# One core, a hybrid decoder block: queries and keys stored two heads at a time, head loads from a high/low layout, gate squares in tiles of their own

## The chip, the cores and the metric

The kernel runs on one core of a Trainium2 chip, in one launch. The metric is the device time of one execution in microseconds (us). Below, PE is TensorE (matmuls), DVE is VectorE, ACT is ScalarE, POOL is GpSimd, and SP is the engine that issues nearly all DMAs. A DMA issued on SP or ACT goes through that queue's share of the core's 16 DMA engines. P is 128, the number of partitions. "Landing" is the time from the issue of a DMA to the moment when its last byte is there.

## What is computed

One decoder block on x of 1024 tokens by 1024 channels, float32. Cut to what matters here:

```python
xn = rmsnorm(h, norm_mix_g)
proj = xn @ w_in                      # q, k, v (8 heads x 64), u, vg (512 each), 8 forget gates
log_f = log_sigmoid(proj[..., G_END:] + b_forget)
att = forgetting_attention(q, k, v, log_f)   # softmax(q k / 8 + c_q - c_k, causal) v; c = cumsum(log_f)
uv = gelu(proj[..., V_END:G_END])
sg = u * (causal 128x128 mix of rmsnorm(vg, per group of 64))
h = h + concat(att, sg) @ w_out
h = h + conv_ffn(rmsnorm(h, norm_ffn_g))     # 1024 -> 5632, width-3 convolution, silu gate, 2816 -> 1024
out = rmsnorm(h, norm_final_g)
```

## The kernel before

Float32 products are made from a high and a low part: a value is cast to a shorter format (high), the rest is the low part, and three matmuls (high x high, high x low, low x high) make one product. The big products are also split by Strassen's scheme in 2x2 blocks, hence names such as A11, S2, T4 for sums of blocks. The work runs in stages:

- 0 to 100 us: the gate half of the first projection (`tmul`, `tprod`; matmuls at L542) with x transposed, which comes in by `load_x` and a first tile `xg` (first 512 columns of x and the gain). `own` makes the parts of x. The weights `wuv` come through SP, the first through ACT's queue.
- 100 to 200 us: forget gates (`forget`, L745 to L774, and `forget_sums`), then four query and key steps (`qk_step`, L887 to L931; matmuls in `product`, L691). Step i makes the transposed queries and keys of heads 2i and 2i+1: tiles of 128 partitions by 1024 tokens. `emit` (L832 to L839) scales them, splits them and stores both parts to DRAM, half a row (512 tokens) at a time. Between the steps' parts, `gate(n)` runs a few pieces of `gate_work` (L799 to L821): squares of the gate half into a "pt" tile (ACT), sums over groups (DVE, L806), square root, and the two multiplications of each tile (L818, L820).
- 200 to 400 us: the values' product (L542), the spatial mix (L971 to L973), and eight heads of attention. Head h needs A (queries, high and low in 128 partitions), B (keys, high and low), B2 (keys, low and high) and ck (the forget sums, the same in each partition). `head_loads` (L852 to L860) brings them by five DMAs into tiles with tags "x1" and "x2", two of each, so that the loads of one head can run while another is computed. `logits` (L1051, L1052) needs all of A, B and B2 for its first block. Beside the heads, PE makes the gated half's output product piece by piece (`Gated`, L1167): each unit of 128 tokens loads a piece of x (L1148) into one of two halves of a tile, adds into it and stores it (L1178) to `hpd`.
- 400 to 1060 us: the rest of the output product, the FFN in blocks, the final norm.

DRAM holds the queries and keys as `qd` and `kd`, shape [8, 2, 64, 1024]: head, high or low, dimension, token. A head's A and B are one contiguous block of 512 KB there.

The order of the instructions on each engine is set by a planner, class `Pace` (L33 to L336): it is given each instruction's cost (`cost`, L143) and a due time worked back from PE, and lists the instructions of each engine in the order in which they would run (`run`, L278). The program then keeps that order; each engine works in order, and waits only where data or a tile require it. So a change of the costs moves instructions on all engines.

Of the kernel before, what the change touches and what calls it, by code (L numbers as in the profile page):

```python
# [14 lines left out]
P = 128  # L15
# [17 lines left out]
class Pace:  # L33
# [109 lines left out]
    def cost(self, i, eng):  # L143

        def size(a):
            n = 1
            for s, c in list(a.ap)[1:]:
                n *= c
            return n

        ins = [a for a in i.ins if getattr(a, "bass_ap", None) is not None]
        outs = [a for a in i.outs if getattr(a, "bass_ap", None) is not None]
        sb = lambda a: a.bass_ap.tensor.name in self.slot and not self.psum(a)
        n = size(outs[0]) if outs else 1
        kind = type(i).__name__
        if "DMA" in kind:
            b = max(size(a) * list(a.ap)[0][1] * 4 for a in ins + outs)
            return 60 if eng == "SP" else 270, b / 330.0 + (1700 if b > 1 << 16 else SMALL), b / 330.0
        if eng == "PE":
            m = size(ins[0])  # L160
            w = size(ins[1])
            exact = "float32r" not in str(ins[0].dtype) and "float32" in str(ins[0].dtype) and not i.is_transpose
            c = 4 * max(m / 2.4, 25) + 230 if exact else max(m / 2.4 + 13.4, w / 1.2 + 2)
            return c, m / 2.4 + 176, 0
        ptr = sum(1 for a in ins if size(a) == 1 and n > 1)
        if eng == "DVE":
            if getattr(i, "is_tensor_tensor_scan", False):
                return 2.1 * n + 100, 2.1 * n + 180, 0
            if "Custom" in kind:
                return n / .96 + 212, n / .96 + 292, 0  # L170
            if "Reduce" in kind:
                return size(ins[0]) / .96 + 70, size(ins[0]) / .96 + 150, 0
            if "Reciprocal" in kind:
                return 150 + 6 * n, 150 + 6 * n, 0
            full = [a for a in ins if size(a) > 1 or n == 1]
            if "TensorTensor" not in kind and len(full) < 2 and not ptr:
                d = n / (1.92 if all(sb(a) for a in ins + outs) else .96) + 150
            else:
                d = n / .96 + 146 + (60 if ptr else 0)
            return d - 80, d, 1 if sum(1 for a in full if size(a) > 8 and sb(a)) >= 2 else 0  # L180
        if eng == "ACT":
            d = n / 1.2 + (160 if any(self.psum(a) for a in ins) else 195) + 100 * ptr
            return (d + 95, d + 190, 0) if len(outs) > 1 else (d - 100, d, 0)
        if "TensorTensor" in kind:
            return 2.0 * n + 160, 2.17 * n + 180, 1
        return .85 * n + 180, .85 * n + 180, 1
# [91 lines left out]
    def run(self, ops, succ, due):  # L278
# [6 lines left out]
        port = {"DVE": 0.0, "POOL": 0.0}  # L285
        order = {e: [] for e in can}
        start = [0.0] * n
        bus, table, done, end = 0.0, 0, 0, 0.0
        for k in range(n):
            if not left[k]:  # L290
                can[ops[k][1]].append(k)
        while done < n:
            pick = None
            for e, ks in can.items():
                if not ks:
                    continue
                f = max(free[e], bus - BACKLOG) if e == "SP" else free[e]
                soon = min(max(f, ready[k]) for k in ks)
                k = min((k for k in ks if ready[k] <= soon + LOOK[e]), key=lambda k: (due[k], k))
                s = max(f, ready[k])  # L300
                if pick is None or s < pick[0]:
                    pick = (s, k)
            s, k = pick
            i, e, (cad, lat, x), deps, fn = ops[k]
            turn = e == "TURN"
            can[e].remove(k)
            if fn and fn != table:
                s += 1283 if table else 0
                table = fn
            if e in port and x:  # L310
                s = max(s, port["POOL" if e == "DVE" else "DVE"])
                port[e] = s + cad
            dma = "DMA" in type(i).__name__
            free[e] = s + cad
            if dma:
                bus = max(s + 300, bus) + x
                fin = bus + lat - x - 200
            else:
                fin = s + lat
            start[k] = s  # L320
            end = max(end, fin)
            if not turn:
                order[e].append(k)
            done += 1
            for q in succ[k]:
                r = s if turn or ops[q][1] == "TURN" else s + cad if ops[q][1] == e and not dma else fin + HOP
                if r > ready[q]:
                    ready[q] = r
                left[q] -= 1
                if not left[q]:  # L330
                    can[ops[q][1]].append(q)
        return order, start, end


SLACK, BACKLOG, SMALL = 30000.0, 3000.0, 4500.0
LOOK = {"PE": 0.0, "DVE": 0.0, "ACT": 0.0, "POOL": 0.0, "SP": 0.0, "TURN": 0.0}  # L336


# [1 line left out]
def block_kernel(ctx: ExitStack, tc: tile.TileContext, xT, xtok, wuv, wv, wqk, wf, cpk, xg, bfv,  # L340
# [81 lines left out]
    bcol = cst.tile([64, 2], F32, name="bcol")  # L422


    qd = drm.tile([8, 2, 64, 1024], F32, name="qd")
    kd = drm.tile([8, 2, 64, 1024], F32, name="kd")
    rbd = drm.tile([8, P], F32, name="rbd")
    ncd = drm.tile([8, 1024], F32, name="ncd")
    zd = drm.tile([8, 1024], F32, name="zd")
# [34 lines left out]
    def gk(k, neg=False):  # L464
        return (ng1 if neg else g1)[:, k:k + 1]

    def xr(n, k):
        return RAW[n][k // 2][:, k % 2, 0:512]

    def load_x(n, k, row, hf):  # L470
        sp.dma_start(out=xr(n, k), in_=xT[row * P:(row + 1) * P, hf * 512:hf * 512 + 512])
# [12 lines left out]
    def own(n, src, k, row, cuts=(0, 512), g=None):  # L484

        g = gk(row) if g is None else g

        for a, b in zip(cuts, cuts[1:]):
            act.activation(xs(n, 0, k)[:, a:b], src[:, a:b], AF.Copy, scale=g)
        dve.scalar_tensor_tensor(out=xs(n, 1, k), in0=src, scalar=g, in1=f32(xs(n, 0, k)),  # L490
                                 op0=ALU.mult, op1=ALU.subtract)

    def hl_of(n, j, src):
        act.copy(x2(n, 0, j), src)
# [6 lines left out]
    gb = []  # L501
    for k in range(4):
        if k == 0:
            sp.dma_start(out=RAW["x11"][0][:, 0, :], in_=xg)
        else:
            load_x("x11", k, k, 0)
        (sp if k else act).dma_start(out=ua[k][:, 0, :], in_=wuv[k, :, 0, :])
    for k in range(4):
        load_x("x21", k, 4 + k, 0)
        sp.dma_start(out=ua[k][:, 1, :], in_=wuv[k, :, 1, :])  # L510
# [43 lines left out]
    for k in range(4):  # L554
        w = tsplit(ua[k][:, 0, :], hi_eng="act" if k else "dve")
        if k == 0:
            graw = RAW["x11"][0][:, 0, 512:520]
            own("B11", xr("x11", 0), 0, 0, (0, 128, 512), graw[:, 0:1])
            dve.tensor_copy(g1, graw)
            dve.tensor_scalar(out=ng1, in0=g1, scalar1=-1.0, scalar2=None, op0=ALU.mult)  # L560
        else:
            own("B11", xr("x11", k), k, k)
        tmul(B, w, "B11", k, True, apart=(k == 0))
    for k in range(4):
        own("B21", xr("x21", k), k, 4 + k)
        tmul(S, tsplit(ua[k][:, 1, :]), "B21", k, True)
    for m in range(4):
        act.copy(vgt[0][:, m, :], B[m])
    for j in range(2):
        dve.tensor_tensor(out=tmp[j][0], in0=RAW["x11"][j][:, :, 0:512], in1=RAW["x12"][j], op=ALU.subtract)  # L570


    def values_low(k):
# [171 lines left out]
    def forget():  # L745
# [16 lines left out]
        for hf in range(2):  # L762
# [7 lines left out]
            zh = zr[:, hf * 512:hf * 512 + 512]  # L770
            act.copy(zh, ps[32:40, :])
            dve.tensor_tensor(out=zh, in0=ps[0:8, :], in1=zh, op=ALU.add)
            pool.tensor_tensor(out=zh, in0=zh, in1=rb[0:8, hf * 512:hf * 512 + 512], op=ALU.mult)
        sp.dma_start(out=zd, in_=zr)  # L774

    def forget_sums():
# [19 lines left out]
    gms = cst.tile([P, 64], F32, name="gms")  # L796
    gg = []

    def gate_work():  # L799

        for hf in (1, 0):
            for t in (0, 2):
                sq = sb("pt", [P, 2, 512])
                act.activation(sq, vgt[hf][:, t:t + 2, :], AF.Square)
                r = gms[:, hf * 32 + t * 8:hf * 32 + t * 8 + 16]
                dve.tensor_reduce(out=r, in_=sq.rearrange("p t (g d) -> p (t g) d", d=64), axis=AX.X, op=ALU.add)  # L806
# [19 lines left out]
        for _ in range(n):  # L826
            next(gw, None)

    gate(2)
    tq, tk = sb("G", [P, 2, 1024]), sb("G", [P, 2, 1024])  # L830

    def emit(t, dst, i, scale, parts):  # L832
        for o in parts:
# [1 line left out]
                                     op0=ALU.mult, op1=ALU.mult)  # L835
            act.copy(t[:, 0, o].bitcast(F32R), t[:, 1, o])
            dve.tensor_tensor(out=t[:, 1, o], in0=t[:, 1, o], in1=t[:, 0, o], op=ALU.subtract)
            for j in range(2):
                sp.dma_start(out=dst[2 * i + j].rearrange("s d t -> d s t")[:, :, o], in_=t[j * 64:(j + 1) * 64, :, o])  # L839

    vgs = []

# [9 lines left out]
    def head_loads(h):  # L852
        ab, nb = sb("x1", [P, 2, 1024], F32R), sb("x2", [P, 2, 1024], F32R)
        A, B, ck, B2 = ab[:, 0, :], ab[:, 1, :], f32(nb[:, 0, :]), nb[:, 1, :]
        sp.dma_start(out=f32(A), in_=qd[h].rearrange("s d t -> (s d) t"))
        sp.dma_start(out=f32(B), in_=kd[h].rearrange("s d t -> (s d) t"))
        sp.dma_start(out=f32(B2[0:64, :]), in_=kd[h, 1])
        sp.dma_start(out=f32(B2[64:128, :]), in_=kd[h, 0])
        sp.dma_start(out=ck, in_=ncd[h:h + 1, :].to_broadcast((P, 1024)))
        return A, B, ck, B2  # L860

# [936 lines left out]
def layouts(inp):  # L1798
# [18 lines left out]
    wos = w_out[512:].reshape(2, 2, P, 2, 512).transpose(3, 0, 2, 1, 4)  # L1817

    wu = g["w_up"][0].reshape(2, 4, P, 2, NFF, P).transpose(4, 2, 3, 0, 1, 5)[:, :, ::-1].reshape(NFF, P, 4, 512)
    r = {"xT": x.T, "xtok": x, "wuv": uv, "wv": wv, "wqk": qk, "wf": wf, "cpk": cpk, "xg": np.concatenate([x.T[:P, :512], g["norm_mix_g"][0].reshape(8, P).T], axis=1),  # L1820
         "bfv": np.repeat(g["b_forget"][0], 8).reshape(64, 1), "ggain": g["gmlp_norm_g"][0].reshape(1, 512),
         "g2r": g["norm_ffn_g"][0].reshape(1, 1024), "gfr": g["norm_final_g"].reshape(1, 1024),
         "wsp": g["w_spatial"][0].transpose(2, 0, 1), "woa": woa, "wos": wos, "wup": wu, "wdn": g["w_down"][0]}
# [17 lines left out]
```

## Time and profile before

| What | us |
|---|---|
| median of three runs (1061.94, 1062.12, 1063.27) | 1062.12 |
| the profiled execution's own time | 1062.15 |
| its span (first to last instruction) | 1060.4 |
| landing of a head's A load (512 KB), median | 4.1 |
| landing of its B load (512 KB), median | 5.6 |
| landing of one half of B2 (256 KB), median | 6.7 |
| landing of its ck load (512 KB), median | 7.5 |
| landing of a queries' store (256 KB, 16 of them), median | 8.5 |
| landing of a keys' store (256 KB, 16 of them), median | 3.7 |

The 1.75 us between the span and the time of the execution lie outside the instructions. In the profile's rows an engine's line is "start, duration, engine, line, operation, out<-in, count", with the idle time before it and what ended it in brackets. In the table of waits a row has the total, the number of times and the longest. In the rows by stage each engine has its busy time and number of instructions, then come the granted PE clock (1.00 is full), the share of time that the 16 DMA engines were busy, and GB/s. DMA packets are what one DMA engine moves at once (a row of 4 KB, say) and, of 4 bytes each, the ones that announce that an engine's share is done.

### The profile page before, as it was taken

What the parts mean: (1) busy time and instruction counts of PE and PEld (TensorE: products, weight loads), DVE (VectorE), ACT (ScalarE), POOL (GpSimd) and SP (SyncE); (2) the same over time, 40 slices, a digit from 0 to 9 for tenths busy, and PEclk for the clock granted to TensorE, in tenths of its full rate; (3) what the DMA queues carried; (4) which work ended last, traced back from release to release, by engine and by line L of the source; (5) the groups of instructions that cost most, each with busy time, mean ns of one, the idle gap of its engine ahead of it and who ended that gap; (6) DMA issues with size and microseconds to landing.
All of it is one profiled execution on the core that took longest, in us unless ns stands there. A gap on an engine that the chain in (4) does not pass through costs nothing.

```text
span 1060.4 us, 14175 instructions
## 1 busy us (share of the span) xinstructions
PE 1046.9 (99%) x4865; PEld 863.3 (81%) x4865; DVE 912.9 (86%) x1381; ACT 574.3 (54%) x1005; POOL 248.4 (23%) x214
## 2 busy tenths in 40 slices
PE   9999989999999999999999999999999999999997
PEld 6888768788888888888888888888888888888885
DVE  5996788998888869999999999999998877697774
ACT  6657354567776746754445444454443554454653
POOL 0002323132452250063343442433422000000000
PEclk9999999999999999999999999999999999999999
DMA  9243336886675355224324232242322997333342
GB/s 340 85 134 119 92 106 174 293 253 194 189 220 169 100 192 187 78 72 139 109 100 129 100 121 79 100 140 74 115 89 91 330 348 254 99 97 102 109 160 89
DMA packets 65032, 158.22 MB, mean 149 GB/s; under 512 B 7664, under 2 KB 8248, under 8 KB 64960
## 3 DMA queue, kind: packets, MB, share of 16 engines
q1 hardware_dynamic: 64384, 156.23, 45.3%
q10 hardware_dynamic: 576, 1.09, 0.3%
q8 instruction: 38, 0.62, 0.3%
q14 instruction: 34, 0.28, 0.1%
HBM read 114.98 MB, written 42.31 MB: 148 GB/s over the span
## 4 chain that ended last, share of the span: by engine, by line
PE 90%; DVE 4%; DMA 3%; issue 1%; ACT 1%; SPq 0%; DVEq 0%; ACTq 0%
PE s L1496 22%; PE b L1496 16%; PE s L1684 11%; PE b L1684 8%; PE s L542 6%; PE b L542 5%; PE fl L1167 4%; PE po L1091 3%; PE tr L1072 3%; PE lg L1052 2%; PE lg L1051 2%; DMA qd<-G 1%; PE b L691 1%; PE b L1407 1%; PE b L1405 1%; PE b L1406 1%
## 5 line engine op out<-in xcount | busy, mean ns | idle before, releaser
L1496 PE MATMUL s<-xT,whb 128*128 128x512 f32 x804 | 189.4, 389 | 0.0
L1496 PEld LDWEIGHTS s<-xT,whb 128*128 128x128 f32 x804 | 150.9, 188 | 31.6 <-DVE whb L446 0.3
L1496 PE MATMUL b<-xB,wha 128*128 128x512 f32 x528 | 126.7, 389 | 0.0
L1684 PE MATMUL s<-whb,wha 128*128 128x512 f32 x528 | 120.2, 389 | 0.0
L1684 PEld LDWEIGHTS s<-whb,wha 128*128 128x128 f32 x528 | 99.1, 188 | 20.5
L1496 PEld LDWEIGHTS b<-xB,wha 128*128 128x128 f32 x528 | 99.0, 188 | 20.4
L440 ACT CAST whb<-sg 128x512 fp32r<-128x512 f32 x82 | 50.6, 620 | 94.6 <-PE s L1496 84.4
L440 ACT CAST wha<-sg 128x512 fp32r<-128x512 f32 x77 | 47.9, 622 | 98.8 <-PE b L1684 45.4
L1684 PE MATMUL b<-whb,wha 128*128 128x512 f32 x396 | 90.2, 389 | 0.0
L446 DVE TENSOR_TENSOR wha<-sg,wha 128x512 fp32r<-128x512 f32 x77 | 53.0, 689 | 39.9 <-ACT wha L440 39.8
L1684 PEld LDWEIGHTS b<-whb,wha 128*128 128x128 f32 x396 | 74.3, 188 | 15.4
L1385 POOL TENSOR_TENSOR sg<-raw,raw 128x512 f32<-128x512 f32 x20 | 40.5, 2023 | 143.4 <-DVE whb L446 143.4
L446 DVE TENSOR_TENSOR whb<-sg,whb 128x512 fp32r<-128x512 f32 x82 | 61.5, 761 | 3.1 <-ACT whb L440 3.0
L1496 PE MATMUL s<-xB,whb 128*128 128x512 f32 x264 | 63.5, 389 | 0.1
L1167 PE MATMUL fl<-whl,H 128*128 128x512 f32 x192 | 62.7, 406 | 0.0
L1496 PE MATMUL b<-xT,whb 128*128 128x512 f32 x252 | 60.7, 389 | 0.0
L1078 ACT CAST pt<-tr 128x512 fp32r<-128x512 f32 (+2 forms) x96 | 45.6, 475 | 25.9 <-PE tr L1072 19.4
L1083 DVE TENSOR_TENSOR pt<-tr,pt 128x512 fp32r<-128x512 f32 (+1 forms) x96 | 51.9, 552 | 7.8 <-ACT pt L1078 7.2
L1496 PEld LDWEIGHTS s<-xB,whb 128*128 128x128 f32 x264 | 49.5, 188 | 10.8 <-DVE h L1567 0.6
L1383 POOL TENSOR_TENSOR sg<-raw 128x512 f32<-128x512 f32 x20 | 37.1, 1857 | 81.6 <-DMA raw<-wup 61.5
L1496 PEld LDWEIGHTS b<-xT,whb 128*128 128x128 f32 x252 | 47.3, 188 | 9.8
L446 DVE TENSOR_TENSOR wha<-raw,wha 128x512 fp32r<-128x512 f32 x44 | 48.8, 1117 | 0.0
(373 smaller groups left out, 2276.2 us busy)
## 6 DMA issues: line engine op xcount, KB each, us to landing
raw<-wup SPq DMA_DIRECT2D x44, 512.0 KB, 3.7
sg<-hx SPq DMA_DIRECT2D x77, 256.0 KB, 2.7
hx<-hs SPq DMA_DIRECT2D x44, 256.0 KB, 2.2
hx<-ca SPq DMA_DIRECT2D x33, 256.0 KB, 2.4
xT<-wdn SPq DMA_DIRECT2D x28, 256.0 KB, 5.3
raw<-wqk SPq DMA_DIRECT2D x8, 512.0 KB, 3.6
qd<-G SPq DMA_DIRECT2D x16, 256.0 KB, 8.5
kd<-G SPq DMA_DIRECT2D x16, 256.0 KB, 3.7
```

The source lines that it names most:

```text
L440: act.copy(h, src)
L446: return eng.tensor_tensor(out=l, in0=src, in1=f32(h), op=ALU.subtract)
L542: pe.matmul(banks[m], xs(n, xi, k)[:, ms], w[:, wi, :], start=(first and k == 0 and c == 0), stop=(k == 3 and c == 2), skip_group_check=True)
L1072: pe.transpose(ps[:, (q - 4 * hf) * P:(q - 4 * hf + 1) * P], self.t[q][:, k * P:(k + 1) * P], ident)
L1078: act.copy(pt[:, 0, o:512], ps[:, o:512])
L1083: dve.tensor_tensor(out=pt[:, 1, o:512], in0=ps[:, o:512], in1=f32(pt[:, 0, o:512]), op=ALU.subtract)
L1091: pe.matmul(self.po[hf][:, o:512], lhs, pt[:, s, o:512], start=(k == 0 and s == 0), stop=(k == 4 * hf + 3 and s == 1), skip_group_check=True)
L1167: pe.matmul(self.bank, sgT[k][:, xi, ts_], self.w[hf, k][:, wi, :], start=(k == 0 and i == 0), stop=(k == 3 and i == 2))
L1383: pool.tensor_tensor(out=s[0], in0=a21, in1=a22, op=ALU.add)
L1385: pool.tensor_tensor(out=s[2], in0=a21, in1=a11, op=ALU.add)
L1496: pe.matmul(ps, w[:, wi, ks], xb[:, xi, k, :], start=(first and n == 0), stop=(n == 11), skip_group_check=True)
L1684: pe.matmul(banks[bk + m], xh[:, xi, ms], wh[:, wi, :], start=(first and p_ == 0 and n == 0), stop=(p_ == NP - 1 and n == 2), skip_group_c ...
```

## The change

- `qd` becomes [2, 4, P, 1024] (high or low, pair of heads, both heads' dimensions, token), `kd` [3, 4, P, 1024], with the keys' high part a second time as third plane. `emit` stores both parts of two heads by one transfer of 128 partitions, and the keys' high part by one more: 24 stores for 32.
- `head_loads` takes A from planes 0 and 1 of `qd`, B from planes 0 and 1 of `kd`, B2 from planes 1 and 2, each by one transfer of 128 partitions: four loads a head for five. The DRAM side of each is then [2 planes, 64 rows, 1024].
- The gate's squares go to tiles of tag "G" that are used for the queries and keys afterwards, and all of `gate_work` is recorded before the first step.
- The forget gates' last multiplication moves from POOL to DVE. At the start, the gain and the first 128 columns come in a transfer of their own, the first weights come through SP, the other 384 columns behind them, and the low part of x is made piece by piece.
[...]

```diff
-            return 60 if eng == "SP" else 270, b / 330.0 + (1700 if b > 1 << 16 else SMALL), b / 330.0
+            x = b / (380.0 if len(o) == 2 else 280.0)
+            return 400 if plain or b < 1 << 17 else 620, x + (1900 if b > 1 << 16 else 3000), x
...
-    qd = drm.tile([8, 2, 64, 1024], F32, name="qd")
-    kd = drm.tile([8, 2, 64, 1024], F32, name="kd")
+    qd = drm.tile([2, 4, P, 1024], F32, name="qd")
+    kd = drm.tile([3, 4, P, 1024], F32, name="kd")
...
     for k in range(4):
         if k == 0:
-            sp.dma_start(out=RAW["x11"][0][:, 0, :], in_=xg)
+            sp.dma_start(out=RAW["x11"][0][:, 0, 0:136], in_=xg)
+            sp.dma_start(out=ua[k][:, 0, :], in_=wuv[k, :, 0, :])
+            sp.dma_start(out=RAW["x11"][0][:, 0, 136:520], in_=xT[0:P, P:512])
         else:
             load_x("x11", k, k, 0)
-        (sp if k else act).dma_start(out=ua[k][:, 0, :], in_=wuv[k, :, 0, :])
+            sp.dma_start(out=ua[k][:, 0, :], in_=wuv[k, :, 0, :])
...
-        tmul(B, w, "B11", k, True, apart=(k == 0))
+        tmul(B, w, "B11", k, True, apart=False)
...
-            pool.tensor_tensor(out=zh, in0=zh, in1=rb[0:8, hf * 512:hf * 512 + 512], op=ALU.mult)
+            dve.tensor_tensor(out=zh, in0=zh, in1=rb[0:8, hf * 512:hf * 512 + 512], op=ALU.mult)
...
+            sqs = early_g()                      # sb("G", [P, 4, 512])
             for t in (0, 2):
-                sq = sb("pt", [P, 2, 512])
+                sq = sqs[:, t:t + 2, :]
...
-    gate(2)
+    for _ in gw:
+        pass
+    gn[0] -= 2
...
-            for j in range(2):
-                sp.dma_start(out=dst[2 * i + j].rearrange("s d t -> d s t")[:, :, o], in_=t[j * 64:(j + 1) * 64, :, o])
+            sp.dma_start(out=dst[0:2, i].rearrange("s r t -> r s t")[:, :, o], in_=t[:, :, o])
+            if dst is kd:
+                sp.dma_start(out=dst[2, i, :, o], in_=t[:, 0, o])
...
-        sp.dma_start(out=f32(A), in_=qd[h].rearrange("s d t -> (s d) t"))
-        sp.dma_start(out=f32(B), in_=kd[h].rearrange("s d t -> (s d) t"))
-        sp.dma_start(out=f32(B2[0:64, :]), in_=kd[h, 1])
-        sp.dma_start(out=f32(B2[64:128, :]), in_=kd[h, 0])
+        for t, d in ((A, qd[0:2]), (B, kd[0:2]), (B2, kd[1:3])):
+            sp.dma_start(out=f32(t), in_=d[:, h // 2, h % 2 * 64:h % 2 * 64 + 64, :])
```

The order on SP around the loads of the first head, before. `G` is the tile of queries or keys that `emit` stores, `x` the tiles of the head loads, `raw` weights of the values:

```order
55 L839 DMA kd<-G_110_1002 64x2x512 x4
56 L839 DMA qd<-G_109_1001 64x2x512 x2
57 L866 DMA raw_1589<-wv 128x1024
58 L866 DMA raw_1587<-wv 128x1024
59 L839 DMA qd<-G_109_1001 64x2x512 x2
60 L855 DMA x_168_1530<-qd 128x1024
61 L856 DMA x_168_1530<-kd 128x1024
62 L857 DMA x_169_1531<-kd 64x1024
63 L858 DMA x_169_1531<-kd 64x1024
64 L859 DMA x_169_1531<-ncd 128x1024
65 L839 DMA qd<-G_109_1001 64x2x512 x2
```

The same place now:

```order
70 L854 DMA qd<-G_110_1029 128x2x512
71 L854 DMA kd<-G_111_1030 128x2x512
72 L874 DMA x_167_1524<-ncd 128x1024
73 L856 DMA kd<-G_111_1030 128x512
74 L873 DMA x_166_1523<-kd 128x1x1024
75 L854 DMA qd<-G_110_1029 128x2x512
76 L873 DMA x_167_1524<-kd 128x1x1024
77 L873 DMA x_166_1523<-qd 128x1x1024
78 L1019 DMA pt_1631<-vd 128x1024
79 L856 DMA kd<-G_111_1030 128x512
80 L854 DMA kd<-G_111_1030 128x2x512
```

The forget sums' load and the keys' load B now stand ahead of the loads B2 and A, and a store of queries stands between them; two stores of keys come behind.

The order on SP over one head's time in the attention, before. `hpd<-t` stores a finished unit of the gated product, `t<-xtok` loads a unit's piece of x, `t<-rsd` brings back a head's sums:

```order
105 L855 DMA x_390_2561<-qd 128x1024
106 L856 DMA x_390_2561<-kd 128x1024
107 L857 DMA x_391_2562<-kd 64x1024
108 L858 DMA x_391_2562<-kd 64x1024
109 L859 DMA x_391_2562<-ncd 128x1024
110 L1178 DMA hpd<-t_192_1647 128x512
111 L1148 DMA t_192_1647<-xtok 128x512
112 L1113 DMA t_378_2513<-rsd 64x1024
113 L1178 DMA hpd<-t_192_1647 128x512
114 L1148 DMA t_192_1647<-xtok 128x512
115 L855 DMA x_451_2825<-qd 128x1024
```

The same head's time now:

```order
113 L873 DMA x_388_2549<-qd 128x1x1024
114 L873 DMA x_388_2549<-kd 128x1x1024
115 L873 DMA x_389_2550<-kd 128x1x1024
116 L874 DMA x_389_2550<-ncd 128x1024
117 L1193 DMA hpd<-t_190_1638 128x512
118 L1163 DMA t_190_1638<-xtok 128x512
119 L1128 DMA t_376_2501<-rsd 64x1024
120 L1193 DMA hpd<-t_190_1638 128x512
121 L1163 DMA t_190_1638<-xtok 128x512
122 L873 DMA x_449_2812<-qd 128x1x1024
```

Four loads stand where five stood, two halves of B2 having become one; the stores, the pieces of x and the sums between one head's loads and the next keep their order.

More of the change, by code (lines that the diff above doesn't have):

```diff
@@ L157, in cost @@
             b = max(size(a) * list(a.ap)[0][1] * 4 for a in ins + outs)
-            return 60 if eng == "SP" else 270, b / 330.0 + (1700 if b > 1 << 16 else SMALL), b / 330.0
+            o, f = list(outs[0].ap), list(ins[0].ap)
+            plain = o[0][1] == P and len(o) == 2 and f[0][0] != 0
+            x = b / (380.0 if len(o) == 2 else 280.0)
+            return 400 if plain or b < 1 << 17 else 620, x + (1900 if b > 1 << 16 else 3000), x
         if eng == "PE":
@@ L179, in cost @@
                 d = n / .96 + 146 + (60 if ptr else 0)
-            return d - 80, d, 1 if sum(1 for a in full if size(a) > 8 and sb(a)) >= 2 else 0
+            quick = "TensorTensor" not in kind and len(full) < 2 and not ptr and n > 64 and all(sb(a) for a in ins + outs)
+            return d - 80, d, 1 if quick or sum(1 for a in full if size(a) > 8 and sb(a)) >= 2 else 0
         if eng == "ACT":
@@ L287, in run @@
         start = [0.0] * n
-        bus, table, done, end = 0.0, 0, 0, 0.0
+        bus, table, done, end = 0.0, None, 0, 0.0
         for k in range(n):
@@ L306, in run @@
             can[e].remove(k)
-            if fn and fn != table:
-                s += 1283 if table else 0
+            if fn and fn != table or table is None and e == "ACT" and "DMA" not in type(i).__name__:
+                s += 1283
                 table = fn
@@ L315, in run @@
             if dma:
-                bus = max(s + 300, bus) + x
-                fin = bus + lat - x - 200
+                bus = max(s + cad, bus) + x
+                fin = bus + lat - x
             else:
@@ L332, in run @@
         return order, start, end
-SLACK, BACKLOG, SMALL = 30000.0, 3000.0, 4500.0
+SLACK, BACKLOG = 30000.0, 3000.0
 LOOK = {"PE": 0.0, "DVE": 0.0, "ACT": 0.0, "POOL": 0.0, "SP": 0.0, "TURN": 0.0}
@@ L465, in gk, with xraw @@
         return (ng1 if neg else g1)[:, k:k + 1]
+    def xraw(n, j):
+        return RAW[n][j][:, :, 8:520] if n == "x11" else RAW[n][j]
     def xr(n, k):
-        return RAW[n][k // 2][:, k % 2, 0:512]
+        return xraw(n, k // 2)[:, k % 2, :]
     def load_x(n, k, row, hf):
@@ L489, in own @@
             act.activation(xs(n, 0, k)[:, a:b], src[:, a:b], AF.Copy, scale=g)
-        dve.scalar_tensor_tensor(out=xs(n, 1, k), in0=src, scalar=g, in1=f32(xs(n, 0, k)),
-                                 op0=ALU.mult, op1=ALU.subtract)
+            dve.scalar_tensor_tensor(out=xs(n, 1, k)[:, a:b], in0=src[:, a:b], scalar=g,
+                                     in1=f32(xs(n, 0, k))[:, a:b], op0=ALU.mult, op1=ALU.subtract)
     def hl_of(n, j, src):
@@ L556, in block_kernel @@
         if k == 0:
-            graw = RAW["x11"][0][:, 0, 512:520]
+            graw = RAW["x11"][0][:, 0, 0:8]
             own("B11", xr("x11", 0), 0, 0, (0, 128, 512), graw[:, 0:1])
@@ L569, in block_kernel @@
     for j in range(2):
-        dve.tensor_tensor(out=tmp[j][0], in0=RAW["x11"][j][:, :, 0:512], in1=RAW["x12"][j], op=ALU.subtract)
+        dve.tensor_tensor(out=tmp[j][0], in0=xraw("x11", j), in1=RAW["x12"][j], op=ALU.subtract)
     def values_low(k):
@@ L797, in block_kernel, with early_g @@
     gg = []
+    def early_g():
+        return sb("G", [P, 4, 512])
     def gate_work():
         for hf in (1, 0):
+            sqs = early_g()
             for t in (0, 2):
-                sq = sb("pt", [P, 2, 512])
+                sq = sqs[:, t:t + 2, :]
                 act.activation(sq, vgt[hf][:, t:t + 2, :], AF.Square)
@@ L1819, in layouts @@
     wu = g["w_up"][0].reshape(2, 4, P, 2, NFF, P).transpose(4, 2, 3, 0, 1, 5)[:, :, ::-1].reshape(NFF, P, 4, 512)
-    r = {"xT": x.T, "xtok": x, "wuv": uv, "wv": wv, "wqk": qk, "wf": wf, "cpk": cpk, "xg": np.concatenate([x.T[:P, :512], g["norm_mix_g"][0].reshape(8, P).T], axis=1),
+    r = {"xT": x.T, "xtok": x, "wuv": uv, "wv": wv, "wqk": qk, "wf": wf, "cpk": cpk, "xg": np.concatenate([g["norm_mix_g"][0].reshape(8, P).T, x.T[:P, :P]], axis=1),
          "bfv": np.repeat(g["b_forget"][0], 8).reshape(64, 1), "ggain": g["gmlp_norm_g"][0].reshape(1, 512),
```

## The prediction

> **What bounds the kernel now.** I read the page first, then the windows, then TensorE's waits, and last SP's timeline and the DMA issues.
>
> ```profile
> span 1060.4 us, 14175 instructions
> PE 1046.9 (99%) x4865; PEld 863.3 (81%) x4865; DVE 912.9 (86%) x1381; ACT 574.3 (54%) x1005; POOL 248.4 (23%) x214
> PE 90%; DVE 4%; DMA 3%; issue 1%; ACT 1%; SPq 0%; DVEq 0%; ACTq 0%
> ```
>
> TensorE is busy for 99% of the span, and the chain that ended last is 90% TensorE. So work moved between other engines gains nothing by itself; the change can take at most TensorE's few idle microseconds, but it can add any number. By stages (busy time of PE, DVE, ACT, POOL, then clock, DMA share, GB/s):
>
> ```profile
> 100.00:200.00 100.00, 96.67 (x420) 76.07 (x419) 83.82 (x122) 47.76 (x78) 29.31 (x22) 1.00 0.50 144
> 200.00:300.00 100.00, 99.34 (x564) 83.66 (x564) 87.91 (x214) 73.54 (x163) 33.31 (x56) 1.00 0.71 215
> 300.00:400.00 100.00, 99.95 (x560) 84.22 (x559) 79.81 (x180) 67.10 (x148) 39.22 (x47) 1.00 0.55 173
> ```
>
> The stretch from 100 to 200 us (queries, keys, gate) loses 3.3 us of TensorE, the attention from 200 to 400 us 0.7 us. In the attention the DMA engines are 55 to 71% busy: room, but not much. TensorE's waits name what can be won:
>
> ```profile
> PE b L542 <- DVE wy L444: 1.4, 1, 1.4
> PE s L691 <- DVE G L915: 1.3, 1, 1.3
> PE s L691 <- DVE whl L446: 0.8, 1, 0.8
> PE s L542 <- DVE G L929: 0.6, 1, 0.6
> PE b L691 <- ACT whl L440: 0.6, 1, 0.6
> PE s L691 <- DVE wy L446: 0.4, 1, 0.4
> PE s L691 <- DVE G L896: 0.2, 1, 0.2
> ```
>
> The last six, 3.9 us, lie between 150 and 202 us; the first is the start.
>
> **The gains, part by part.** The gate's squares get tiles of their own and the gate's work runs before the first query step, the stores become 24 instead of 32, and the forget product goes from POOL to DVE. All this aims at the 3.9 us. It can take all or nothing of them: the moved VectorE work is the same work, and VectorE has 16 us free in that stretch. In the new order TensorE still finds VectorE close behind at the third matmul block of steps 0, 2 and 3. I take 1.6 us as coming back (bounds 0 and 3.9), so 2.3 are won. At the start, gain and first 128 columns come first and the weights' low parts later; of the 1.4 us wait I take 0.6 (bounds 0 and 1.4). The second store of the keys' high part adds 8 x 256 KB of writing and is awaited only by the head loads; I cost it at nothing unless those loads bind, and then it is in them. Together -2.9 us, between -5.3 and 0.
>
> **The head loads.** Here lies the size. Each head needs A (queries), B and B2 (keys) whole before its first logits. Before, they come from one contiguous block in DRAM, with 128 or 64 as the outermost dimension; now each is `d[:, h // 2, ...]`, whose outermost dimension in DRAM is 2 (high, low), then 64 rows. What decides on how many of the 16 DMA engines a transfer runs? Two short windows, each with the packets of one transfer alone:
>
> ```profile
> DMA packets 16, 0.03 MB, mean 12 GB/s; under 512 B 8, under 2 KB 8, under 8 KB 16
> zd<-whl SPq DMA_DIRECT2D x1, 32.0 KB
> ...
> DMA packets 144, 0.52 MB, mean 131 GB/s; under 512 B 16, under 2 KB 16, under 8 KB 144
> h2d<-pt SPq DMA_DIRECT2D x1, 512.0 KB, 2.6
> ```
>
> A transfer of 128 rows of 4 KB leaves 128 packets of data and 16 small ones that close it; one of 8 rows leaves 8 and 8. So an engine closes its own share, and 8 outermost entries gave 8 engines, not 16. By the same count 2 outermost entries give 2 engines, with 256 KB on each. No transfer before has an outermost dimension of 2, and in all of them the outermost counts of source and destination agree, so the trace doesn't say whether the destination's 128 partitions could still spread these loads over 16; that is a rival below.
>
> [...]
>
> The pace of one engine has two rows:
>
> ```profile
> 418.00:419.00 1.00, 1.00 (x6) 0.81 (x5) 1.00 (x3) 0.97 (x4) 0.00 (x0) 1.00 1.01 406
> q1 hardware_dynamic: 64384, 156.23, 45.3%
> ...
> hpd<-t SPq DMA_DIRECT2D x16, 256.0 KB, 3.6
> ```
>
> With all 16 fully busy on rows of 4 KB, 406 / 16 = 25.4 GB/s each. Over the whole run 156.23 MB in 45.3% of 16 x 1060.4 us is 20.3. So 262,144 bytes take 10.3 us, at worst 12.9; I take 10.3, since with 14 engines nearly idle little competes. Landing adds 2.6 - 1.3 = 1.3 us (the 512 KB store above against its moving time). Three loads a head: 30.9 us on the same two engines, and whatever SP issues later has its share on these two queued behind. What a head has now:
>
> ```profile
> 249.83 0.32 SPq L855 DMA_DIRECT2D x<-qd  x1
> ...
> 251.85 0.58 SPq L859 DMA_DIRECT2D x<-ncd  x1
> 252.53 0.38 SPq L1148 DMA_DIRECT2D t<-xtok  x1
> 255.13 0.32 SPq L1178 DMA_DIRECT2D hpd<-t  x1
> ...
> 260.74 0.45 SPq L1113 DMA_DIRECT2D t<-rsd  x1
> ...
> 325.17 0.32 SPq L855 DMA_DIRECT2D x<-qd  x1
> ```
>
> Loads start when the head before last has had its last logits; from 249.83 to 325.17 are four heads, 18.8 us each. 30.9 us of transfer can't hide under 18.8 us of work. The period then goes by the queue. From one head's loads landed to the next head's: the ncd load (512 KB on 16 engines, 1.3) and the hpd store behind it (0.7) land; SP, which stood at the xtok load waiting for that store's tile, issues xtok, rsd and the next hpd (0.4 + 0.5 + 0.4); that store lands (3.6); the next xtok, which waits for it, goes out (0.4) and the next head's loads behind it: 7.3, then 1.3 + 30.9. That is 39.5 us, or 20.7 more than 18.8. If the queue's chain hides altogether, 33.5.
>
> The first three heads have other conditions:
>
> ```profile
> 178.23 3.03 SPq L839 DMA_DIRECT2D kd<-G  x4
> 185.47 1.23 SPq L839 DMA_DIRECT2D qd<-G  x2
> ...
> 205.26 0.22 PE L1051 MATMUL lg<-x 128*128 128x128 f32 x1
> 206.85 2.88 PE L542 MATMUL s<-whl,x 128*128 128x512 f32 x12
> ...
> 231.41 0.39 PE L1052 MATMUL lg<-x,x 128*128 128x512 f32 x1
> ```
>
> Head 0: B is issued behind the third step's key stores (181.3), B2 and A behind a queries' store (186.7) and so behind B on the two engines: 181.3 + 1.3 + 30.9 + 1.3 for that store's and the last key store's shares = 215. First logits stand at 205.3: 10 us of stall. Head 1: its second tile is free when the 12 matmuls after the first logits end, 209.7, now 219.7; 1.3 + 30.9 + 1 later is 253, needed at 231.9 + 10: 11 more. Head 2: issued after head 0's last logits, so the two engines come straight from head 1's loads: 253 + 31.9 = 285, needed at 249.8 + 21: 14 more. Heads 3 to 7: 5 x 20.7 = 103.5. In all 138.5 us.
>
> A last cost shows only at the start, where matmuls follow idle time:
>
> ```profile
> 0.84 3.60 PE L405 MATMUL s<-const-bfloat16-1.0 128*128 128x512 bf16 x10 [0.84 <-PEq L1833]
> 6.46 5.53 PE L542 MATMUL b<-wy,V 128*128 128x512 f32 x23 [0.17 <-DVE wy L446]
> ```
>
> 0.36 us a matmul against 0.24: if each of 8 stalls leaves TensorE cold like that, some 1.3 us a stall, 10 in all; nothing if not. I take 5.
>
> **The sum**, against the profiled execution's own 1062.15 us (span 1060.4 and 1.75 around it; the median of the three runs is 1062.12): 1062.15 - 2.9 + 138.5 + 5 = 1202.7, or 1203.
>
> **Rivals.** *The loads spread over all 16 engines* (the destination's count decides). Then their cost is that of the old ones, 1.3 us of moving for 512 KB, and only the gains stay: 1062.15 - 2.9 = 1059.2, between 1056.8 and 1062.2, not slower. For it: partitions are what every load before was divided by. Against it: the 8-row store shows that a count under 16 isn't made up. It decides if the changed kernel's packets close with 16 per head load. Chance 0.2.
>
> *Two engines at the mean pace*, 12.9 us a load, since SP's other transfers and the stores' 2 KB rows go through them too. Heads 0 to 2 then lose 18, 19 and 22, the period is 47.3: 5 x 28.5 = 142.5; with 10 for the cold clock and no gain, 1062.15 + 201.5 + 10 = 1274. For it: from 200 to 300 us the share of 0.71 moved 215 GB/s, 18.9 an engine. Against: that is with all 16 busy. Chance 0.17.
>
> *Two engines, the SP chain hidden*: period 33.5, 5 x 14.7 = 73.5 and 35, with full gains and no cold clock 1062.15 + 108.5 - 5.3 = 1165. That is the lower end of my forecast, which with it has 0.63.
>
> **How the numbers follow.** The range has to hold 8 in 10: forecast and slow pace, 0.63 + 0.17. Below 1165 the stalls of the first heads could be 10 us smaller, so 1155; above 1274 a little, 1280. A difference of 0.2% is 2.1 us, about what a measurement here can tell from none. The first rival gives 0.12 faster, 0.06 within and 0.02 slower; all else is slower: 0.82.
>
> **What would show it.** In the changed kernel's windows from 200 to about 500 us TensorE should be idle for half of the time, ended by the DMA of the head tile (x); head loads should be 38 to 41 us apart and land 31 us or more after issue; DMA share should fall to some 0.3 while two engines run. Stage 400 to 1060 should only shift. I am wrong on the cause if head loads land in 4 to 8 us as now, and on the period if they lie 33 or 47 us apart. Of the gains, waits of lines L691 between 100 and 205 us should sum to about 1.6.

## The result and the profile after

| | before | after |
|---|---|---|
| median, us | 1062.9 (1061.94 to 1065.61, 5 runs) | 1231.11 (1229.16 to 1231.76, 5 runs) |
| profiled execution, us | 1062.15 | 1231.76 |
| its span, us | 1060.4 | 1230.0 |

The changed kernel takes 1.158 times as long, interval 1.156 to 1.160. Forecast were 1203 and a range from 1155 to 1280. The page of the changed kernel, with the span, the engines' busy time and the chain that ended last:

```profile
span 1230.0 us, 14127 instructions
PE 1068.2 (87%) x4865; PEld 878.6 (71%) x4865; DVE 914.0 (74%) x1384; ACT 579.6 (47%) x1007; POOL 249.1 (20%) x212
PE 75%; DMA 19%; issue 3%; SPq 1%; DVE 1%; ACT 1%; POOL 0%; POOLq 0%; ACTq 0%
```

In the chain PE's share falls from 90% to 75% of the span, and DMA's rises from 3% to 19%. PE's busy time also rose by 21.3 us, with the same 4865 matmuls; the other 148.3 us of the longer span are idle time. By stages:

```profile
0.00:100.00 100.00, 98.45 (x423) 78.73 (x424) 79.60 (x125) 66.25 (x106) 6.81 (x13) 1.00 0.50 179
100.00:200.00 100.00, 99.77 (x440) 79.81 (x438) 91.87 (x138) 52.58 (x85) 28.34 (x21) 1.00 0.47 159
200.00:300.00 100.00, 50.60 (x253) 41.60 (x252) 38.63 (x94) 33.78 (x71) 10.55 (x16) 0.75 0.36 115
300.00:400.00 100.00, 58.78 (x299) 49.10 (x300) 41.66 (x109) 36.76 (x86) 17.66 (x31) 0.74 0.25 84
...
600.00:700.00 100.00, 100.00 (x441) 82.28 (x440) 98.56 (x113) 51.51 (x71) 36.81 (x21) 1.00 0.31 103
```

Up to 200 us the change gains: 3.1 us of PE in the stretch from 100 to 200 us, 0.8 in the 100 us ahead of it. From 200 to 512 us, the attention, PE is idle for half of the time, and the granted clock is 0.75 and 0.74 in the two stretches shown. From 600 us on all is as before, only later. PE's waits, and the stalls one by one:

```profile
PE lg L1067 <- DMA x<-kd: 47.9, 5, 9.8
PE lg L1066 <- DMA x<-kd: 28.4, 4, 11.3
PE fl L1182 <- POOL whl L450: 27.2, 1, 27.2
PE lg L1066 <- DMA x<-qd: 27.2, 2, 21.4
PE po L1106 <- DVE pt L1098: 22.2, 1, 22.2
PE s L700 <- DVE G L911: 0.2, 1, 0.2
```

```profile
221.59 0.44 PE L1066 MATMUL lg<-x 128*128 128x128 f32 x1 [21.43 <-DMA x<-qd]
256.36 0.55 PE L1066 MATMUL lg<-x 128*128 128x256 f32 x1 [5.74 <-DMA x<-qd]
266.77 0.58 PE L1067 MATMUL lg<-x,x 128*128 128x256 f32 x1 [9.85 <-DMA x<-kd]
292.72 0.44 PE L1066 MATMUL lg<-x 128*128 128x128 f32 x1 [5.55 <-DMA x<-kd]
302.67 0.47 PE L1067 MATMUL lg<-x,x 128*128 128x128 f32 x1 [9.51 <-DMA x<-kd]
344.79 0.47 PE L1106 MATMUL po<-pt,V 128*128 128x128 f32 x1 [22.24 <-DVE pt L1098]
...
511.97 0.47 PE L1067 MATMUL lg<-x,x 128*128 128x128 f32 x1 [9.21 <-DMA x<-kd]
```

Of the waits of line L691 (now L700), 0.2 us are left. In their place the first logits of most heads wait for A (x<-qd), then B and B2 (x<-kd), which land one after the other, some 10 us apart (256.36 to 266.77, 292.72 to 302.67). The two rows that name VectorE (22.2 us) and GpSimd (27.2 us) hang on DMAs as well: VectorE had waited 24.3 us for a piece of x (t<-xtok), and GpSimd 32.7 us for the forget sums (x<-ncd), both issued behind head loads.

### The profile page after: what moved, and what is told of

Read it like the earlier page. It is cut to its first block, busy times and chain, and to the rows that moved or that the text cites. A ratio compares the mean times of both kernels' runs of the same rounds, so it can differ in the third digit from the quotient of the medians.

```text
span 1230.0 us, 14127 instructions
## 1 busy us (share of the span) xinstructions
PE 1068.2 (87%) x4865; PEld 878.6 (71%) x4865; DVE 914.0 (74%) x1384; ACT 579.6 (47%) x1007; POOL 249.1 (20%) x212
## 4 chain that ended last, share of the span: by engine, by line
PE 75%; DMA 19%; issue 3%; SPq 1%; DVE 1%; ACT 1%; POOL 0%; POOLq 0%; ACTq 0%
PE s L1511 20%; PE b L1511 14%; DMA x<-kd 14%; PE s L1699 10%; PE b L1699 7%; PE b L551 4%; PE s L551 4%; PE s L700 3%; DMA x<-qd 3%; PE b L700 3%; PE fl L1182 2%; PE po L1106 1%; DMA hpd<-t 1%; PE tr L1087 1%; PE b L1422 1%
## 5 line engine op out<-in xcount | busy, mean ns | idle before, releaser
L1182 PE MATMUL fl<-whl,H 128*128 128x512 f32 x192 | 70.8, 451 | 27.2 <-POOL whl L450 27.2
L1066 PE MATMUL lg<-x 128*128 128x512 f32 (+3 forms) x96 | 41.0, 428 | 55.5 <-DMA x<-kd 28.4
L1067 PE MATMUL lg<-x,x 128*128 128x512 f32 (+3 forms) x96 | 37.1, 386 | 47.9 <-DMA x<-kd 47.9
L1106 PE MATMUL po<-pt,V 128*128 128x512 f32 (+1 forms) x192 | 52.4, 369 | 22.2 <-DVE pt L1098 22.2
L1074 DVE CUSTOM_DVE_ANT_0 gg<-lg,gg,lim 128x128 f32<-128x128 f32 (+1 forms) x16 | 6.6, 414 | 86.5 <-POOL gg L1057 62.8
L1400 POOL TENSOR_TENSOR sg<-raw,raw 128x512 f32<-128x512 f32 x20 | 37.3, 1864 | 159.9 <-DVE whb L450 159.9
L1066 PEld LDWEIGHTS lg<-x 128*128 128x128 f32 x96 | 20.6, 214 | 59.2 <-issue 50.7
L1182 PEld LDWEIGHTS fl<-whl,H 128*128 128x128 f32 x192 | 38.7, 215 | 33.2 <-POOL whl L450 27.5
```

Source lines behind the costliest of these rows:

```text
L1066: pe.matmul(ps[:, 0:e - c], self.A[:, qs], self.B[:, c:e], start=True, stop=False)
L1106: pe.matmul(self.po[hf][:, o:512], lhs, pt[:, s, o:512], start=(k == 0 and s == 0), stop=(k == 4 * hf + 3 and s == 1), skip_group_check=True)
L1182: pe.matmul(self.bank, sgT[k][:, xi, ts_], self.w[hf, k][:, wi, :], start=(k == 0 and i == 0), stop=(k == 3 and i == 2))
L1400: pool.tensor_tensor(out=s[2], in0=a21, in1=a11, op=ALU.add)
```

## Experiments

### Are two engines the cause?

The head loads of the changed kernel, by halves (`halves`):

```diff
+        r = slice(h % 2 * 64, h % 2 * 64 + 64)
...
-            sp.dma_start(out=f32(t), in_=d[:, h // 2, h % 2 * 64:h % 2 * 64 + 64, :])
+            for s in range(2):
+                sp.dma_start(out=f32(t)[s * 64:s * 64 + 64, :], in_=d[s, h // 2, r, :])
```

> The changed kernel with each of A, B and B2 loaded by two transfers of 64 partitions, one per plane (outermost 64 in DRAM), so six of 256 KB for three of 512 KB; layout, stores, gate work and planner costs stay changed. Theory (a transfer runs on as many DMA engines as its outermost dimension allows, 2 in the changed kernel): the loads spread again, land in 4 to 8 us, and the time is 1057 to 1062. Rival A (one load over two planes that lie 2 MB apart is slow in DRAM): also 1057 to 1062, since no load spans two planes. Rival B (the new order or the issue on SP holds the loads up): still above 1150.

One transfer again, but with the rows outermost (`woven`):

```diff
-            sp.dma_start(out=f32(t), in_=d[:, h // 2, h % 2 * 64:h % 2 * 64 + 64, :])
+            sp.dma_start(out=f32(t), in_=d[:, h // 2, r, :].rearrange("s r t -> r s t"))
```

> The changed kernel with the three loads as one transfer each, but the source read row by row, high and low in turn (outermost 64, then 2): the partitions of A, B and B2 hold high and low woven, all three alike, and the logits are sums over the partitions. Theory: 16 engines, 1057 to 1062, four loads a head, no later than with the halves. Rival A (two planes 2 MB apart in one transfer are slow): stays near 1231, since it reads the same bytes of the same planes in one transfer. Rival B: above 1150.

`halves` took 1056.27 us, a little under its forecast, 0.9942 of before (0.9929 to 0.9956); `woven` 1057.01, 0.9943 (0.9931 to 0.9956). So the whole loss hangs on the order of two dimensions in the source of three loads. `woven` reads the same bytes of the same planes in as many transfers, which leaves nothing of rival A, and both keep the new order, which leaves nothing of rival B. Both are faster than the kernel before, by some 6 us, and than the changed one, by some 174. The packets of the changed kernel, then those of `woven`, show the engines:

```profile
DMA packets 65608, 160.32 MB, mean 130 GB/s; under 512 B 7088, under 2 KB 7928, under 8 KB 65536
```

```profile
DMA packets 65944, 160.32 MB, mean 152 GB/s; under 512 B 7424, under 2 KB 8264, under 8 KB 65872
```

The megabytes are the same; the small packets that close a share are 336 fewer in the changed kernel, 14 for each of 24 head loads: 2 engines close where 16 did. And a stretch of the changed kernel in which a head load moves alone:

```profile
258.00:266.00 8.00, 0.00 (x0) 0.00 (x0) 0.00 (x0) 0.00 (x0) 0.00 (x0) 0.50 0.13 52
```

Every engine of the core idles; the DMA share is 0.13, two sixteenths, at 52 GB/s, 26 for each of two.

### One and two such loads a head

```diff
+        sp.dma_start(out=f32(A), in_=qd[0:2, h // 2, r, :])      # outermost 2; in two_of_three B as well
+        for t, d in ((B, kd[0:2]), (B2, kd[1:3])):               # in two_of_three B2 alone
+            for s in range(2):
+                sp.dma_start(out=f32(t)[s * 64:s * 64 + 64, :], in_=d[s, h // 2, r, :])
```

> The changed kernel with A still one load with outermost 2, B and B2 by halves of 64 partitions. Theory: the two engines carry 10.3 us of load a head under 18.8 us of work, so it is hidden but for the first heads: 1058 to 1075. Rival A (each such load delays by itself, hidden or not): a third of the 169 us, about 1115.

> The changed kernel with A and B as loads with outermost 2, B2 by halves. Theory: 20.6 us of transfer a head do not fit under 18.8, and SP's chain comes on top (the changed kernel's period is 42.7 against 30.9 of transfer): period 24 to 32, 1085 to 1150. A cost in proportion to the number of such loads would give about 1172.

`one_of_three` took 1110.65 us (1.045, 1.0433 to 1.0467), `two_of_three` 1170.19 (1.1012, 1.0997 to 1.1027). Both miss: from none to three such loads a head the steps are 54, 60 and 61 us, nearly in proportion. The theory that a transfer costs nothing as long as it is shorter than the head's work has fallen. Of the 55 us between the profiled executions of `halves` and `one_of_three`, 43 are idle time of TensorE and 12 more busy time with the same matmuls. The rows of `one_of_three` on SP, and what SP waited for between 215 and 345 us:

```profile
260.57 0.54 SPq L873 DMA_DIRECT2D x<-qd  x1
...
264.45 0.43 SPq L1166 DMA_DIRECT2D t<-xtok  x1
277.66 0.32 SPq L1196 DMA_DIRECT2D hpd<-t  x1
```

```profile
SPq L1166 <- DMA x<-qd: 33.8, 3, 12.3
SPq L1166 <- DMA hpd<-t: 28.6, 7, 5.0
SPq L1196 <- DMA x<-qd: 12.7, 1, 12.7
```

SP issues nothing from 264.9 to 277.66, and waits for x<-qd, the A load, though neither the store nor the loads of x pieces use it. VectorE then waits 10.6 us for a piece of x, and TensorE 8.6 us for VectorE.

### Is it the order in SP's queue?

A second theory: the small transfers stand behind the head load in the queue. So the stores, then also the x pieces, go through ACT's queue.

```diff
-                sp.dma_start(out=hpd[tt, :, hf * 512:hf * 512 + 512], in_=hs)
+                act.dma_start(out=hpd[tt, :, hf * 512:hf * 512 + 512], in_=hs)
...
-            sp.dma_start(out=self.hs[u], in_=xtok[...])          # the *_both_act kernels alone
+            act.dma_start(out=self.hs[u], in_=xtok[...])
```

> The kernel with A alone as a load with outermost 2 (1110.7 us), and the stores of the gated units (hpd) issued on ACT's queue, not SP's, so that they do not stand behind the head loads. Theory (the 10 us of a load on two engines are hidden themselves, but SP's stores and the loads that wait for them stand behind it in the same queue): SP's loads of x pieces go out without the wait of 12 us, and the time falls to 1057 to 1085. Rival (each such load costs its share by itself, some 55 us, whatever stands behind it): 1105 to 1115.

> The changed kernel (three loads with outermost 2) with the hpd stores on ACT's queue. Theory: the part of the period that is SP's chain (42.7 less 32.2 of transfer and landing) shrinks by the stores' waits, the transfers stay: period 34 to 39, so 1185 to 1212. Rival: unchanged, 1225 to 1235.

> As the kernel with A alone on two engines and the hpd stores on ACT (1107.1 us), with the loads of x pieces for the gated units on ACT's queue too. The stores alone brought 3.5 us, so what stands behind the head load must be the load of x, for which VectorE waits (10.6 us once, and with it TensorE 8.6). Theory (queue order, not the transfer): 1057 to 1080, with some loss to ACT, which now waits for the stores' landing. Rival (the load costs some 54 us by itself, through any queue): 1100 to 1112.

> The changed kernel with stores and x pieces of the gated units on ACT's queue. Theory: of a period of 42.7 the three transfers (30 at 26 GB/s an engine) stay, SP's chain and the waits behind them go: 33 to 38, so 1165 to 1207. Rival: 1220 to 1231.

`one_hpd_act` 1107.11 us (1.0417, 1.0401 to 1.0434), `one_both_act` 1111.5 (1.0447, 1.0425 to 1.0468); `after_hpd_act` 1226.7 (1.1556, 1.1532 to 1.158), `after_both_act` 1223.98 (1.1511, 1.1491 to 1.1531). The queue is worth 3.5 us or nothing with A alone, and 4 or 7 of 168 with all three: this theory has fallen too. With both on ACT, it is ACT that stands (waits of `one_both_act`):

```profile
ACT pt L1096 <- DMA x<-kd: 23.5, 3, 8.4
ACT pt L1096 <- DMA x<-qd: 14.0, 2, 8.2
```

ACT's cast of the attention weights uses nothing of these loads. What stands ahead of it in ACT's order is a DMA:

```profile
256.28 0.34 ACTq L1166 DMA_DIRECT2D t<-xtok  x1
256.66 0.27 ACT L1096 CAST pt<-tr 128x128 fp32r<-128x128 f32 x1 [7.37 <-DMA x<-kd]
```

The load of a piece of x goes out at 256.28. The 7.37 us for which ACT stood before its cast are put down to x<-kd, a head load of which neither that piece nor the cast uses anything. The 12.7 us of SP in `one_of_three` are of the same kind. So an engine does not wait only where data or a tile require it, as the text ahead of the prediction has it. What ties these transfers to the head loads, no run shows. But the waits are there in SP's queue as in ACT's (33.8 and 12.7 us for x<-qd on SP in `one_of_three`, 23.5 for x<-kd and 14.0 for x<-qd on ACT in `one_both_act`), and that would explain why moving transfers to ACT only moves the wait.

The chain that ended last in `one_of_three` names a second cause. Three of its transfers, with start and time in flight:

```profile
264.45 18.66 DMA t<-xtok
...
348.42 18.12 DMA x<-ncd
...
374.76 17.16 DMA x<-kd
```

None of them is an A load, and none was held back: they had been issued, and were 17 to 19 us in flight, where before a piece of x landed in 2.9 us, the forget sums in 7.5 and a half of B2 in 6.7 (medians). The piece of x issued at 264.45 is the one for which VectorE waits 10.6 us, and TensorE 8.6 for VectorE. From 273 to 277 us, while it is in flight, the DMA share is 0.12 to 0.13, as where a head load moved alone. So this stall fits the step of the prediction by which what is issued later has its share queued on the two engines, and no wait ahead of an issue is needed for it.

No experiment separates the two causes, so how much of the 54 us a load is owed to waits of the first kind, and how much to the shares that other transfers have on the two engines, stays open.

### What the rest of the change brings

Undone one at a time: the gate's part from `woven`, the old planner costs in `woven` (what `cost` gives a DMA, in the diff ahead of the prediction, and the rules of `run`), the stores from `halves`, and of these only the third plane.

```diff
-                sq = sqs[:, t:t + 2, :]                          # gate_spread, and gate(2) for all of gate_work
+                sq = sb("pt", [P, 2, 512])
...
-            sp.dma_start(out=dst[0:2, i].rearrange("s r t -> r s t")[:, :, o], in_=t[:, :, o])
-            if dst is kd:                                        # no_third drops these two lines alone
-                sp.dma_start(out=dst[2, i, :, o], in_=t[:, 0, o])
+            for j in range(2):                                   # stores64
+                q = slice(j * 64, j * 64 + 64)
+                sp.dma_start(out=dst[0:2, i, q].rearrange("s r t -> r s t")[:, :, o], in_=t[q, :, o])
```

> The woven kernel (1057.0) with the gate's part undone: squares in pt tiles, two pieces ahead, the rest spread over the query steps as before. If the waits of 3.9 us between 150 and 202 came from the gate's work standing late on VectorE, they come back: 1060 to 1061.5. If they came from the stores, it stays at 1057.

> The halves kernel (1056.3) with the stores undone: two stores of 64 partitions for one of 128, no second store of the keys' high part, B2 by halves from planes 1 and 0. If the waits came from late stores (tiles not free), 1058 to 1060; if from the gate, 1056 to 1057.

> The halves kernel (1056.3) without the second store of the keys' high part: B2 by halves from planes 1 and 0, stores of 128 partitions. It tells the two parts of the stores apart: undoing both gave 1065.2. If it was the stores of 64 partitions, 1055.5 to 1057 here; if B2 from two planes, about 1065.

> The woven kernel (1057.0) with the planner's old costs and rules, everything else as changed. If the new costs bring part of the gain, 1058 to 1062; if stores and gate bring all of it, 1056 to 1058.

| | us | of before |
|---|---|---|
| `halves` | 1056.27 | 0.9942 (0.9929 to 0.9956) |
| `no_third` | 1057.54 | 0.9943 (0.9928 to 0.9958) |
| `stores64` | 1065.18 | 1.0029 (1.0019 to 1.004) |
| `woven` | 1057.01 | 0.9943 (0.9931 to 0.9956) |
| `gate_spread` | 1058.83 | 0.9966 (0.9953 to 0.9979) |
| `costs_old` | 1059.46 | 0.996 (0.9945 to 0.9975) |

Undoing the stores costs most: 7.6 us against `no_third`, more than was expected either way, and the gain is gone. The third plane can't be told from nothing. With the gate's part or the costs undone the kernel comes out some 2 us slower, but the intervals just touch or overlap, so neither is clear of the noise. The forget gates' multiplication and the start were not undone. PE's waits of `stores64`, and the stretch where they lie:

```profile
PE s L700 <- DVE G L913: 2.0, 1, 2.0
PE b L988 <- DVE A L997: 1.7, 1, 1.7
PE b L1010 <- DVE A L997: 1.1, 1, 1.1
```

```profile
190.00:195.00 5.00, 2.23 (x7) 0.84 (x6) 4.69 (x12) 1.33 (x2) 1.25 (x4) 0.81 1.05 407
195.00:200.00 5.00, 3.00 (x9) 2.22 (x10) 3.70 (x6) 1.20 (x2) 0.00 (x0) 0.50 0.49 145
```

PE waits 4.8 us for VectorE there, and the granted clock falls to 0.50 in the second stretch. But from 180 to 200 us VectorE itself waits 0.9 us in all, for TensorE and ScalarE, and not for a store. It is late because its order is another: the difference that TensorE waits for (L913) comes at 197.2 us, behind 14 pieces of L997; in `no_third` (L911 there) it comes at 185.5. So the run shows what the stores are worth together with the order that the planner makes for them; that they save time by themselves is not shown.

## Why the prediction was right, point by point

**The number of engines** was the step that decided, and it held: 2 closing packets a load (14 fewer than in `woven`), 52 GB/s, and the loss gone when the rows are put outermost. The trace of before had only shown that a transfer of 8 outermost rows closes with 8 small packets, one of 128 with 16; that the source's 2 count although the destination has 128 is what `woven` adds.

**The pace of an engine**, 10.3 us a load, held: 10.4 and 10.0 us between landings, 26 GB/s. The rival of 12.9 us did not come.

**The first three heads** were forecast at 10, 11 and 14 us of stall, 35 in all; the rows show 21.4, 15.6 and 15.1, 52. Most of the 17 us is head 0's. TensorE came to the first logits at 200.2 us, not 205.3, and so waited 5 us longer; and A, issued at 187.6 where 186.7 was forecast, landed at 221.4 and not 215. What held it so long is not shown.

**The period** of the last five heads was forecast at 39.5 us. From the first logits of head 2 (302.67) to those of head 7 (511.97) it is 41.9:

```profile
302.67:511.97 209.30, 108.39 (x552) 90.33 (x552) 78.69 (x205) 69.02 (x159) 34.31 (x56) 0.73 0.26 87
```

TensorE idles for 100.9 us of it, 20.2 a head, where 20.7 were forecast. So the waits were sized right, and the longer period is busy time: 21.7 us a head, at a mean granted clock of 0.73, for 18.8. The changed kernel's rows on SP for one of these heads:

```profile
306.19 0.51 SPq L873 DMA_DIRECT2D x<-qd  x1
306.75 9.72 SPq L873 DMA_DIRECT2D x<-kd  x2
316.53 9.93 SPq L874 DMA_DIRECT2D x<-ncd  x1
326.55 1.02 SPq L1163 DMA_DIRECT2D t<-xtok  x1
327.67 1.72 SPq L1193 DMA_DIRECT2D hpd<-t  x1
344.40 0.33 SPq L1163 DMA_DIRECT2D t<-xtok  x1
344.83 0.49 SPq L1128 DMA_DIRECT2D t<-rsd  x1
345.41 0.53 SPq L1193 DMA_DIRECT2D hpd<-t  x1
349.33 0.33 SPq L1163 DMA_DIRECT2D t<-xtok  x1
349.71 0.51 SPq L873 DMA_DIRECT2D x<-qd  x1
```

The chain is the one forecast: three loads, a store that lands behind them at 344.4, x piece, sums, store, 3.9 us until that has landed, x piece, next loads, at 349.71. But moved off SP's queue, store and x pieces gain 4 to 7 us in all, not the 4 to 10 a head that I expected of `after_hpd_act` and `after_both_act`. So as far as "the period then goes by the queue" means SP's order, the step fell as a cause, and that 20.7 came so near to 20.2 is in part luck. Something else is as late when SP's chain is gone; the shares on the two engines and the waits for head loads ahead of other DMAs are the candidates that the rows name. The step "30.9 us of transfer can't hide under 18.8 us of work" was right but not the point: 10 us under 18.8 don't hide either, as `one_of_three` shows.

**The clock** was the term most mis-sized, by a factor of four: 5 us (10 at most), from matmuls at the start, against 21.3 us of added busy time. `woven`, with the same matmuls and no such stalls, has 1045.5 us of it, no more than the 1046.9 of before. The changed kernel behind the stall that ended at 302.67, and behind 322.5, where PE fell idle:

```profile
307.00:308.00 1.00, 1.00 (x5) 0.80 (x5) 0.00 (x0) 0.26 (x2) 0.36 (x1) 0.50 0.87 277
308.00:309.00 1.00, 1.00 (x8) 0.91 (x7) 0.63 (x2) 0.26 (x1) 0.00 (x0) 0.94 0.48 127
...
324.00:325.00 1.00, 0.00 (x0) 0.00 (x0) 0.00 (x0) 0.00 (x0) 0.00 (x0) 1.00 0.13 53
325.00:326.00 1.00, 0.00 (x0) 0.00 (x0) 0.00 (x0) 0.00 (x0) 0.00 (x0) 0.59 0.12 49
```

PE fell idle at 322.5, and the granted clock fell to 0.50 some 2.6 us later. Behind the stall before, it had stayed there for 5.4 us of new work. From 200 to 520 us it falls to 0.50 eight times, 2.0 to 5.2 us after PE fell idle, and stays there for 3.8 to 6.0 us behind the last wait of the stall, 39.7 us in all. By an estimate from these, with half the work done at 0.50, half of that, some 20 us, is what the stalls cost beyond themselves; that comes near the 21.3 us.

**The gains** were forecast at 2.9 us (0 to 5.3); with the loads repaired they are 6, 0.57%. `halves` by stages:

```profile
0.00:100.00 100.00, 99.11 (x425) 79.60 (x426) 80.06 (x126) 66.63 (x106) 6.83 (x13) 1.00 0.50 179
100.00:200.00 100.00, 99.67 (x441) 80.01 (x440) 91.11 (x137) 53.59 (x87) 27.85 (x21) 1.00 0.57 185
```

The waits of 100 to 300 us give 3.7 us (99.67 and 100.00 against 96.67 and 99.34; forecast 2.3): next to nothing of them came back, and of the waits at L691, put at 1.6, the changed kernel has 0.2 left. The start can't be told from its 0.6: 1.5 us here (97.61 to 99.11), but `woven`, whose code is the same there, has less than before:

```profile
0.00:100.00 100.00, 97.38 (x419) 77.84 (x420) 78.65 (x125) 65.29 (x104) 6.80 (x13) 1.00 0.50 179
```

The whole gain lies just above the bound of 5.3.

**The sum.** Of the profiled execution's 169.6 us, 148.3 are idle time, where stalls less gains had been put at 135.6, and 21.3 clock for 5. The two misses, 13 and 16, are the 29 us between 1203 and 1231.76. The 13 are 17 too little for the first three heads, less 3 too much for the other five and 2 more of gains.

## What to carry to other kernels

Read the outermost dimension of both sides of every DMA before looking at its bytes: 512 KB with a leading dimension of 2 took 10 us to move, where 16 engines need 1.3 at the 406 GB/s measured, and putting the rows outermost repaired it for nothing, since a sum over partitions doesn't care in which order they stand. A slow transfer isn't free because it is shorter than the work beside it: one load of 10 us a head, beside 18.8 us of work, cost 54 us here. What was issued after it came late (three transfers 17 to 19 us in flight, where before the medians were 2.9 to 7.5), and moving the small transfers to another queue didn't free them (1107.11 and 1111.5 us for 1110.65). And a stall is to be priced with the clock behind it: here it fell to 0.50 after 2.0 to 5.2 us of idle time, and stayed there for 3.8 to 6.0 us of new work.

## What the runs showed of the hardware that was not expected

- SP's own instruction that issues a DMA took some 10 us at many places. In the changed kernel the issue of the forget sums' load (L874) took 0.33 to 17.7 us, median 9.9, in `woven` 0.33 to 0.59, median 0.58. In the rows above, the third head load and the load behind it are issued about 10 us apart, as long as one load moves. The runs with fewer such loads differ: between 300 and 400 us, in `two_of_three` it is the pair of halves of B2, issued behind two of them, that takes 9.1 to 9.6 us, and the forget sums' load 0.6; in `one_of_three` all four halves together take 2.4 us. What such an issue waits for, no run shows.
- The granted clock fell to 0.50 in each of the eight long stalls of the changed kernel, 2.0 to 5.2 us after PE fell idle. It fell with shorter waits as well: in `stores64` it was 0.50 from 195 to 200 us, behind waits of 4.8 us in all, and PE's busy time was 3.6 us more than in `no_third` (1050.6 against 1047.0).
